# Storing the second one-hot of the PEER gate matrix token by token

## The chip, the cores and the metric

The kernel runs on one core of one Trainium2 chip. The metric is the device time of one execution in microseconds (us), from the chip's own clock. The engines are named as the profile names them: PE is TensorE's matrix multiply, PEld its loading of the stationary operand, DVE is VectorE, ACT is ScalarE, POOL is GpSimd, and SP is the engine that here only issues DMAs.

## The reference, cut to what matters

A decoder trunk of two layers (one recurrent, one with latent attention) runs over 512 tokens of width 1024. Each layer ends in a PEER block: every token picks 16 of 16384 tiny experts in each of 8 heads, and the result is a gated sum over the picked experts.

```python
def peer(h, w_q, sub_keys, u_tab, v_tab):
    q = (h @ w_q).reshape(B, S, PEER_HEADS, 2, PEER_HALF)
    s = jnp.einsum('bshpd,hpnd->bshpn', q, sub_keys)
    v1, i1 = lax.top_k(s[..., 0, :], 16); v2, i2 = lax.top_k(s[..., 1, :], 16)
    cand = v1[..., :, None] + v2[..., None, :]       # 16 x 16 per head
    cv, ci = lax.top_k(cand, 16)                      # of the 256
    idx = e1 * 128 + e2;  g = softmax(cv)             # e1, e2: the two key numbers
    act = gelu(h . u_tab[idx])
    return sum(g * act * v_tab[idx])
```

## The kernel before

The kernel does not gather rows for the first 384 tokens. It treats the block as two dense products over all 16384 experts (128 tiles of 128 experts), and multiplies the activations by a **gate matrix** that holds g where a token picked an expert and zero elsewhere. The last 128 tokens are done with gathered rows, in the background. Operands in fp32 are split in a high and a low part, and each product is three matmuls (lines 181, 182 and 183 of the helper `mm3`), so that most of the PE work is on these three lines.

A PEER block has these stages, once in each layer:

1. Queries, key scores and top-k (`pq`, `sc`, lines 914 to 942).
2. **The gate stage** (lines 945 to 978). The key numbers e1 and e2 of each block of 128 tokens are decoded (`decode`, lines 763 to 808, tiles `oh`, `ib`, `e`), transposed so that tokens lie along the free dimension (`gate_prep`, tiles `et`, `gp`), and then `gate_group` is called 24 times, once for 16 tokens each.
3. The V stage (lines 1029 to 1053): for each of 128 expert tiles the activations are weighted and multiplied by a tile of the value table into six accumulators (`acc`), while gathers for the last 128 tokens go on.

For one token the gate matrix over 128 x 128 key pairs is the product of two one-hot matrices over the 128 picks: rows of picks against key number e2 (**o2**, the stationary operand) and rows of picks against key number e1, times g (**pr**, the moving operand, in two fp16 parts). `gate_group` works on 16 tokens as two halves of eight (HT = 8). For each half VectorE makes

- `o1` (line 840): is key number equal to e1, for 128 keys and 8 tokens, 1024 fp16 elements in each partition;
- `pr[1]` (line 841): o1 times the low part of g, on VectorE in the first half and on GpSimd in the second;
- `o2` (line 842): is key number equal to e2;
- `pr[0]` (line 843): o1 times the high part of g.

The profile strips buffer numbers, so both one-hots are named `o` there and the line tells them apart. All four tiles have the shape [128, 2, 128, 4]: two groups, then keys, then four tokens **interleaved** as the innermost dimension. The instruction therefore reads the e2 of four neighbouring tokens as neighbouring elements, and compares them with a table `iota_e` in which each key number stands four times. TensorE then runs 16 matmuls for the half (line 848), each of 128 x 128 x 128 in fp16, and both of its operands step by four elements (8 bytes) from column to column. ScalarE copies each bank of four tokens to `stg` (line 851), and `stg` goes out to a DRAM scratch (line 853) from which the V stage reads it back.

Between the groups the program issues `u_part` (lines 888 to 905): a tile of the first table is loaded, split on ScalarE (line 161, `whi`) and GpSimd (line 162, `wlo`), multiplied on TensorE in 24 matmuls of 384 columns, and passed through GELU. Each call of `gate_group` is followed by the decode steps of later blocks. The last three `u_part` of the stage are held until the last gate matmul (lines 974 and 975).

The order of the instructions on each engine is not the order of the code: a scheduler sets it ahead of time from its own estimate of what each instruction costs. `o2` and `pr` have two buffers each, so VectorE can be two halves ahead of TensorE.

Of the kernel before, what the change touches and what calls it, by code (L numbers as in the profile page):

```python
# [12 lines left out]
F16 = mybir.dt.float16  # L13
# [3 lines left out]
OP = mybir.AluOpType  # L17
# [4 lines left out]
P = 128  # L22
# [16 lines left out]
TG = 16  # L39
# [8 lines left out]
HT = 8  # L48
# [31 lines left out]
class Trunk:  # L80
# [24 lines left out]
    def setup(self):  # L105
        nc, c, io = self.nc, self.consts, self.io
        self.csil = c.tile([P, D], F32, name="csil")
        nc.scalar.dma_start(self.csil, bass.AP(tensor=io["c"].tensor, offset=io["c"].offset, ap=[[0, P], [1, D]]))
        nc.scalar.activation(self.csil, self.csil, AF.Silu)
        self.x = self.state.tile([P, KC, T], F32, name="x")  # L110
        for k in range(0, KC, 2):
            nc.sync.dma_start(self.x[:, k:k + 2, :], io["xT"][:, k:k + 2, :])
        self.vecs = c.tile([P, NV], F32, name="vecs")
        nc.scalar.dma_start(self.vecs, io["vecs"])
        self.cst = c.tile([P, 4], F32, name="cst")
        nc.scalar.dma_start(self.cst, io["cst"])
        ii = c.tile([P, P], I32, name="ii")
        nc.gpsimd.iota(ii, pattern=[[1, P]], base=0, channel_multiplier=-1)
        self.ident = c.tile([P, P], F32, name="ident")
        nc.vector.tensor_scalar(self.ident, ii, 0.0, None, op0=OP.is_equal)  # L120
        self.ones = c.tile([P, 1], F32, name="ones")
        nc.vector.memset(self.ones, 1.0)
        self.iota_e = c.tile([P, P, 4], F16, name="iota_e")
        nc.gpsimd.iota(self.iota_e, pattern=[[1, P], [0, 4]], base=0, channel_multiplier=0,
                       allow_small_or_imprecise_dtypes=True)
        self.iota_m = c.tile([P, TOPK, TOPK], BF, name="iota_m")
        nc.gpsimd.iota(self.iota_m, pattern=[[1, TOPK], [0, TOPK]], base=0, channel_multiplier=0,
                       allow_small_or_imprecise_dtypes=True)
        self.eps = c.tile([P, 1], F32, name="eps")
        nc.vector.memset(self.eps, EPS)  # L130
        self.tiny = c.tile([P, 1], F32, name="tiny")
        nc.vector.memset(self.tiny, 1e-30)
        self.mod = c.tile([P, 112], F32, name="mod")
        self.xscr = self.dram.tile([P, KC, T], F32, name="xscr")
        self.gscr = self.dram.tile([DEPTH, SPILL, P, ND], F32, name="gscr")
        self.rscr = self.dram.tile([P, T], F32, name="rscr")
        self.mscr = self.dram.tile([P, NB, T], BF, name="mscr")
        self.wscr = self.dram.tile([DEPTH, NSG, P, P * TG], F32, name="wscr")
# [686 lines left out]
    def gate_group(self, pool, l, b, sg, et, gp):  # L825
        nc = self.nc
        n4 = HT // 4
        shp = [P, n4, P, 4]
        io = self.iota_e.unsqueeze(1).to_broadcast(shp)
        stg = pool.tile([P, P, TG], F32, name="stg", bufs=2)  # L830
        for t0 in range(0, TG, HT):

            def toks(ap):
                o = sg * TG + t0
                return ap[:, o:o + HT].rearrange("p (a t) -> p a t", t=4).unsqueeze(2).to_broadcast(shp)

            o2 = pool.tile(shp, F16, name="o2", bufs=2)
            o1 = pool.tile(shp, F16, name="o1", bufs=2)
            pr = [pool.tile(shp, F16, name=f"pr{q}", bufs=2) for q in range(2)]
            nc.vector.tensor_tensor(o1, io, toks(et[:, 0, :]), op=OP.is_equal)  # L840
            (nc.gpsimd if t0 else nc.vector).tensor_tensor(pr[1], o1, toks(gp[:, 1, :]), op=OP.mult)  # L841
            nc.vector.tensor_tensor(o2, io, toks(et[:, 1, :]), op=OP.is_equal)  # L842
            nc.vector.tensor_tensor(pr[0], o1, toks(gp[:, 0, :]), op=OP.mult)  # L843
            for a in range(n4):
                wps = self.bank("wps")
                for t in range(4):
                    for q in range(2):
                        last = nc.tensor.matmul(wps[:, t * P:t * P + P], o2[:, a, :, t], pr[q][:, a, :, t],  # L848
                                         start=q == 0, stop=q == 1)
                c = t0 + 4 * a  # L850
                nc.scalar.activation(stg[:, :, c:c + 4].rearrange("p e t -> p t e"),
                                     wps.rearrange("p (t e) -> p t e", t=4), AF.Copy, scale=1.0 / GSCALE)
        nc.scalar.dma_start(self.wscr[l, b * (P // TG) + sg], stg.rearrange("p e t -> p (e t)"))
        return last.ins
# [370 lines left out]
```

## Time and profile before

| | |
|---|---|
| median of three runs | 3260.37 us (3260.09 to 3264.49) |
| span of the profiled execution, first to last instruction | 3255.7 us |
| instructions | 43571 |
| mean granted TensorE clock | 0.967 |
| gate stage, layer 0 | about 490 to 727 us |
| V stage, layer 0 | about 727 to 1620 us |
| gate stage, layer 1 | about 2126 to 2367 us |
| V stage, layer 1 | about 2367 to 3222 us |

The span leaves out what lies ahead of the first and behind the last instruction: the median of the runs is 4.7 us longer than the profiled execution's span, and the profile gives no other time for that execution. "Busy" in the profile is the time from an instruction's start to its end, which includes time in which an engine that has started an instruction is held up inside it. A row of a timeline gives start, duration, engine, line, operation, and the tiles written and read. A row of a view by stages gives the stretch, its length, the busy time and number of instructions of PE, PEld, DVE, ACT and POOL, the granted clock, the DMA share and GB/s.

### The profile page before, as it was taken

To read this page: it belongs to the slowest core of one execution; us is meant where nothing else is said; L and a number is where in the kernel's file an instruction comes from. 1 tells how busy PE (TensorE), PEld (TensorE's weight loads), DVE (VectorE), ACT (ScalarE), POOL (GpSimd) and SP (SyncE) were. 2 spreads that over 40 slices of the span, in tenths; PEclk is the share of its full clock that TensorE was granted. 3 is DMA by queue.
4 is the path that set the end of the run, shared out by engine and by line. 5 is a ranking of instruction groups with operands and counts; after the bars stand their busy time and mean duration, and the time that the engine had idled before them with its cause. 6 is when DMAs were issued, how large, how long until landed. Compare 5 with 4: busy or idle time off the path is not lost. (4 is left out here: it accounts for less than half of the span.)

```text
span 3255.7 us, 43571 instructions
## 1 busy us (share of the span) xinstructions
PE 3027.2 (93%) x15486; PEld 2673.7 (82%) x15486; DVE 2721.5 (84%) x4924; ACT 1401.5 (43%) x1986; POOL 1491.7 (46%) x995
## 2 busy tenths in 40 slices
PE   6778879999999999999988989988999999999998
PEld 4657778898799999999766768878888899999997
DVE  8999999987688888888768968999956888888877
ACT  4543236653333333333456652356543333333333
POOL 5554455651044444444346645656510444444442
PEclk9888989999999999999989999989999999999999
DMA  6443445569899999999512333345698999999994
GB/s 249 147 162 130 145 148 180 186 225 344 274 359 350 328 335 337 349 336 326 178 36 84 100 110 130 112 176 183 218 313 257 315 350 328 336 333 344 341 333 175
DMA packets 319771, 786.55 MB, mean 242 GB/s; under 512 B 30785, under 2 KB 153793, under 8 KB 313153
## 3 DMA queue, kind: packets, MB, share of 16 engines
q1 hardware_dynamic: 226960, 443.61, 40.8%
q0 software_dynamic: 73728, 268.47, 23.1%
q10 hardware_dynamic: 18864, 71.69, 5.6%
q8 instruction: 122, 2.00, 0.2%
q14 instruction: 97, 0.79, 0.1%
HBM read 713.68 MB, written 69.99 MB: 241 GB/s over the span
## 5 line engine op out<-in xcount | busy, mean ns | idle before, releaser
L181 PE MATMUL u<-hh,wlo 128*128 128x384 f32 x2048 | 699.6, 342 | 19.8 <-ACT gact L905 13.2
L183 PE MATMUL u<-hh,whi 128*128 128x384 f32 x2048 | 697.8, 341 | 0.0
L182 PE MATMUL u<-hl,whi 128*128 128x384 f32 x2048 | 696.1, 340 | 0.0
L1110 POOL DMA_INDIRECT grow<-in_u_dram,idx x256 | 334.0, 1305 | 662.4 <-DVE gdot L1114 483.2
L162 POOL TENSOR_TENSOR wlo<-raw,whi 128x1024 fp32r<-128x1024 f32 (+2 forms) x211 | 481.0, 2285 | 271.7 <-ACT whi L161 261.4
L182 PE MATMUL acc<-vl,ah 128*128 128x512 f32 x1536 | 600.6, 391 | 2.3 <-DVE vl L162 2.3
L183 PE MATMUL acc<-vh,ah 128*128 128x512 f32 x1536 | 600.8, 391 | 0.0
L181 PE MATMUL acc<-vh,al 128*128 128x512 f32 x1536 | 592.0, 389 | 2.7 <-DVE mod L151 1.0
L162 DVE TENSOR_TENSOR vl<-vraw,vh 128x1024 fp32r<-128x1024 f32 x256 | 313.6, 1225 | 243.1 <-ACT vh L161 231.0
L1110 POOL DMA_INDIRECT grow<-in_v_dram,idx x256 | 329.1, 1285 | 380.2 <-DVE gacc L1119 259.0
L181 PEld LDWEIGHTS u<-hh,wlo 128*128 128x128 f32 x2048 | 392.9, 192 | 27.8 <-issue 14.0
L161 ACT ACTIVATE whi<-raw 128x1024 fp32r<-128x1024 f32 (+2 forms) x376 | 362.8, 966 | 118.2 <-PE acc L183 66.0
L182 PEld LDWEIGHTS u<-hl,whi 128*128 128x128 f32 x2048 | 392.1, 191 | 6.2
L183 PEld LDWEIGHTS u<-hh,whi 128*128 128x128 f32 x2048 | 391.8, 191 | 0.1
L181 PEld LDWEIGHTS acc<-vh,al 128*128 128x128 f32 x1536 | 288.4, 188 | 61.0 <-ACT vh L161 1.4
L183 PEld LDWEIGHTS acc<-vh,ah 128*128 128x128 f32 x1536 | 288.3, 188 | 60.2
L182 PEld LDWEIGHTS acc<-vl,ah 128*128 128x128 f32 x1536 | 288.3, 188 | 60.0 <-DVE vl L162 3.0
L1114 DVE CUSTOM_DVE_ANT_0 grow<-grow,hn 128x1024 f32<-128x1024 f32 x256 | 307.9, 1221 | 27.2 <-DMA grow<-in_u_dram,idx 26.6
L1119 DVE SCALAR_TENSOR_TENSOR gacc<-grow,gdot,gacc 128x1024 f32<-128x1024 f32 x254 | 325.2, 1280 | 5.5 <-DMA grow<-in_v_dram,idx 4.6
L161 ACT ACTIVATE ah<-gact 128x384 fp32r<-128x384 f32 x240 | 126.2, 526 | 467.8 <-DVE gact L997 327.2
L905 ACT ACTIVATE gact<-u 128x384 f32<-128x384 f32 x176 | 86.5, 491 | 494.0 <-PE u L183 487.6
L161 ACT ACTIVATE vh<-vraw 128x1024 fp32r<-128x1024 f32 x256 | 268.5, 1051 | 42.0 <-DMA vraw<-in_v_dram 23.5
(357 smaller groups left out, 5089.7 us busy)
## 6 DMA issues: line engine op xcount, KB each, us to landing
raw<-in_uT_dram SPq DMA_DIRECT2D x256, 512.0 KB
vraw<-in_v_dram SPq DMA_DIRECT2D x256, 512.0 KB
ada_raw<-in_adaw_dram SPq DMA_DIRECT2D x112, 512.0 KB
wscr<-stg ACTq DMA_DIRECT2D x48, 1024.0 KB
wt<-wscr SPq DMA_DIRECT2D x32, 1536.0 KB
raw<-in_w_pq_dram SPq DMA_DIRECT2D x32, 512.0 KB
gscr<-gsp ACTq DMA_DIRECT2D x64, 192.0 KB
gact<-gscr SPq DMA_DIRECT2D x64, 192.0 KB
```

The costliest lines, as they stand in the source:

```text
L161: nc.scalar.activation(hi, src, AF.Copy)
L162: return (eng or nc.vector).tensor_tensor(lo, src, hi.bitcast(F32), op=OP.subtract)
L181: nc.tensor.matmul(out, al, bh, start=first, stop=False)
L182: nc.tensor.matmul(out, ah, bl, start=False, stop=False)
L183: return nc.tensor.matmul(out, ah, bh, start=False, stop=last)
L905: nc.scalar.activation(gact[t], out[:, :ND], AF.Gelu)
L1110: nc.gpsimd.indirect_dma_start(out=row, out_offset=None, in_=tabs[s], in_offset=bass.IndirectOffsetOnAxis(ap=idx[:, k:k + 1], axis=0))
L1114: nc.vector.tensor_tensor_reduce(row, row, hn, op0=OP.mult, op1=OP.add, scale=1.0, scalar=0.0, accum_out=col)
L1119: nc.vector.scalar_tensor_tensor(acc, row, col, acc, op0=OP.mult, op1=OP.add)
```

## The change

The second one-hot is stored token by token: [128, 8, 128], tokens outside and the 128 key numbers inside. Each matmul then reads its stationary operand with a step of one element. A new table `iota_c` of [128, 128] holds each key number once. The comparison reads that table again for each token, and reads the e2 of one token again for all 128 keys. `o1` and `pr` stay interleaved by four.

```diff
+        self.iota_c = c.tile([P, P], F16, name="iota_c")
+        nc.gpsimd.iota(self.iota_c, pattern=[[1, P]], base=0, channel_multiplier=0,
+                       allow_small_or_imprecise_dtypes=True)
...
-            o2 = pool.tile(shp, F16, name="o2", bufs=2)
+            rows = [P, HT, P]
+            o2 = pool.tile(rows, F16, name="o2", bufs=2)
...
-            nc.vector.tensor_tensor(o2, io, toks(et[:, 1, :]), op=OP.is_equal)
+            o = sg * TG + t0
+            nc.vector.tensor_tensor(o2, self.iota_c.unsqueeze(1).to_broadcast(rows),
+                                    et[:, 1, o:o + HT].unsqueeze(2).to_broadcast(rows), op=OP.is_equal)
...
-                        last = nc.tensor.matmul(wps[:, t * P:t * P + P], o2[:, a, :, t], pr[q][:, a, :, t],
+                        last = nc.tensor.matmul(wps[:, t * P:t * P + P], o2[:, 4 * a + t, :], pr[q][:, a, :, t],
                                           start=q == 0, stop=q == 1)
```

In the changed kernel the lines stand at other numbers: `o1` is line 844, `pr[1]` 845, `o2` 847, `pr[0]` 849, the matmul 854, and `wlo` 165.

## The prediction

> **What bounds the kernel now.** I read the view by stages first, over the stretches in which the changed lines run: the two gate stages, each cut where PE stops having idle time, and the second V stage behind them.
>
> ```profile
> 490.00:686.00 196.00, 176.94 (x1165) 170.18 (x1164) 188.64 (x230) 124.85 (x146) 116.25 (x51) 0.93 0.53 187
> 686.00:727.00 41.00, 40.83 (x281) 39.04 (x280) 34.76 (x28) 25.68 (x30) 23.88 (x10) 1.00 0.67 249
> 2126.00:2307.00 181.00, 158.04 (x1057) 151.16 (x1055) 174.40 (x210) 115.76 (x135) 110.33 (x45) 0.94 0.54 188
> 2307.00:2367.00 60.00, 59.64 (x403) 57.12 (x404) 46.28 (x47) 36.04 (x42) 37.29 (x17) 0.97 0.64 228
> 2367.00:3222.00 855.00, 855.00 (x4212) 764.03 (x4211) 672.47 (x854) 313.88 (x425) 321.17 (x253) 1.00 0.93 322
> ```
>
> In the first and third row PE (first busy column) leaves 19 and 23 us idle, and DVE (third) leaves only 7 us idle in each. In the second and fourth row it is the other way round: PE is full and DVE has 6 and 14 us free. In the last row PE is busy all the time, so a microsecond that the gate stage ends later is a microsecond later at the end. DMA is at 0.53 to 0.67 in the gate stages and bounds nothing there.
>
> The waits of layer 0's stage say whom PE waits for, and the chain that ended last, in order of time, says the same for layer 1 (start, length, engine and line):
>
> ```profile
> PEld L848 <- DVE o L842: 22.4, 13, 6.0
> PE wps L848 <- DVE o L842: 18.5, 11, 5.7
> ```
>
> ```profile
> 2294.32 0.61 DVE o L842
> 2294.93 0.60 DVE o L840
> ...
> 2306.70 0.61 DVE o L842
> 2307.36 2.06 PE wps L848 x16
> ```
>
> The gate matmuls wait for the very instruction that the change touches, and the chain runs along DVE until 2307 us and then along PE. The steps of 0.60 us are the pace of these DVE instructions when nothing holds them up.
>
> But DVE's busy time is not all work. The timeline shows what is in it:
>
> ```profile
> 2187.47 0.68 DVE L842 TENSOR_TENSOR o<-iota_e,et 128x1024 f16<-128x1024 f16 x1
> 2187.87 2.54 POOL L162 TENSOR_TENSOR wlo<-raw,whi 128x1024 fp32r<-128x1024 f32 x1 [2.67 <-ACT whi L161]
> 2188.07 2.89 DVE L840 TENSOR_TENSOR o<-iota_e,et 128x1024 f16<-128x1024 f16 x1
> 2191.10 2.21 POOL L841 TENSOR_TENSOR pr<-o,gp 128x1024 f16<-128x1024 f16 x1 [0.69 <-DVE o L840]
> 2191.48 2.38 DVE L841 TENSOR_TENSOR pr<-o,gp 128x1024 f16<-128x1024 f16 x1
> ```
>
> The DVE instruction at 2188.07 takes 2.89 us where its twin took 0.68: the POOL instruction ends at 2190.41, and DVE ends 0.55 us after it. The same again at 2191.48. So in this stage **DVE and POOL take turns**, one instruction at a time. The shortest of each form show their work without the turn-taking (duration as min/median/max in ns):
>
> ```profile
> L842 DVE TENSOR_TENSOR o<-iota_e,et x96: 677/680/2876, 490.9 to 2358.1; 128x1024 f16<-128x1024 f16 x96
> L841 POOL TENSOR_TENSOR pr<-o,gp x48: 1889/2212/6026, 496.9 to 2357.6; 128x1024 f16<-128x1024 f16 x48
> L162 POOL TENSOR_TENSOR wlo<-raw,whi x28: 2385/2685/6450, 492.8 to 721.3; 128x1024 fp32r<-128x1024 f32 x28
> ```
>
> I add up layer 1's stage by turns. DVE makes 168 one-hots and products (48 + 48 + 48 + 24) at 0.60 = 101 us. POOL makes 24 products at 1.89 = 45 us and some 29 splits at 2.39 = 69 us. The decode's `oh` instructions, about 2.1 us for each of 10 steps by the same pace (an estimate), are 21 us. The sum is 236 us of the 241 between 2126 and 2367. So the stage is filled by these two engines' turns, and the PE-full tails are about full of turns too.
>
> **The change part by part.**
>
> *o2 on DVE, 96 instructions.* The amount of data stays, 1024 fp16 elements. What changes is that one operand now repeats a single element 128 times, and no row of the trace has that on DVE. It is bounded by 0.68 us (the pace is kept) and by the nearest form of as many elements without pairs, a split in fp32:
>
> ```profile
> L162 DVE TENSOR_TENSOR vl<-vraw,vh x256: 1217/1226/1289, 728.9 to 3220.9; 128x1024 fp32r<-128x1024 f32 x128
> L162 DVE TENSOR_TENSOR vl<-v,vh x8: 654/680/692, 1662.6 to 1817.8; 128x512 fp32r<-128x512 f32 x8
> L162 DVE TENSOR_TENSOR yl<-tanh,yh x4: 679/1222/2865, 165.7 to 230.5; 128x512 fp32r<-128x512 f32 x4
> ```
>
> 512 elements of four bytes take 0.680 us, exactly as long as 1024 of two bytes. So DVE moves one 4-byte word per step, and two fp16 neighbours ride in one word. A repeated element has no neighbour to ride with, so I take the unpaired price, 1.226 us: **+0.546 us each**. The third row excludes that the slow form escapes the turns: its 512 fp32 elements take up to 2.87 us. [...]
>
> *Where the 96 lie.* The view by stages for line 842 alone counts them:
>
> ```profile
> 490.00:686.00 196.00, 36.04 (x40) 0.93 0.53 187
> 686.00:727.00 41.00, 7.14 (x8) 1.00 0.67 249
> 2126.00:2307.00 181.00, 28.43 (x36) 0.94 0.54 188
> 2307.00:2367.00 60.00, 16.98 (x13) 0.97 0.64 228
> ```
>
> 76 lie where DVE and POOL alone set the pace: 76 x 0.546 = **+41.5 us**. The other 20 lie in the tails: at most 20 x 0.546 = 10.9 us more, at least nothing if they all fit into the 20 us that DVE has free there. In the compiled order of the changed program PE's `u` matmuls come earlier (29 to 32 between two groups where there were 25 to 28), and the last three to four groups of each layer have none between them. PE then no longer fills the tails, and the turns set the pace to the end. I take 7.5 of the 10.9 us, since some gaps there can be filled.
>
> *The matmuls, 1536 of them.* Their number, columns and moving operand stay. The weight load is a possible gain:
>
> ```profile
> L848 PEld LDWEIGHTS <-o x1536: 112/117/146, 497.4 to 2365.3; 128*128 128x128 f16 x192
> 2234.48 3.96 PE wps L848 x32
> ```
>
> 32 matmuls take 3.96 us with their drain, so about 118 ns from one to the next, as long as one load. The moving operand still steps by 8 bytes, and either may set that pace. The ends are no gain at all and half a load, 59 ns; a loss I exclude, since the same columns are read from neighbouring addresses. The upper end is 1536 x 59 = 91 us of PE time, but in the early stretches PE waits for o2 anyway and only waits longer, and in the tails it is no longer the bound. I count **0**, covered by the turns of DVE and POOL; if that cover were gone (the pairing kept), the 355 gate matmuls of the tails (147 + 208) could give at most 355 x 59 = 21 us. [...]
>
> *The rest.* The iota costs less than its larger sister's 1.20 us (row below), at 1 us into the span, behind the first loads: nothing. `toks` loses one use, at no cost at run time. On SP two `u` loads move ahead of the first read-back of `wscr`, with DMA half free. Behind the slower o2 on DVE wait `pr[0]`, the next o1 and the decode, and POOL's `wlo` and `pr[1]` wait for their turn; that is the cost already counted.
>
> ```profile
> L124 POOL IOTA iota_e<- x1: 1197/1197/1197, 1.0 to 1.0; 128x512 f16 x1
> ```
>
> *Sum.* 41.5 + 7.5 = **+49 us**: the profiled span would go from 3255.7 to 3304.7, and with the 4.7 us by which the median stands above the span, the predicted time is 3260.4 + 49 = **3309 us**.
>
> **The rivals.**
>
> *A. Part of the turns is slack.* If POOL's records are longer than what they really hold (its spans are rough), DVE can slip into the difference. For it: 5 us of layer 1's stage are not in my sum. Against it: DVE ends 0.55 us after POOL each time. With half the price hidden, 96 x 0.546 / 2 = +26: 3286 us.
>
> *B. The pairing is kept*, because the repeated operand costs nothing. Then the edit does not do to DVE what I say, and PE waits as before: 3260 us. For it: no row of the trace has the case.
>
> *C. Faster.* The pairing is kept, and the load halves. Early stretches stay as they are, and the full-PE tails shrink. It decides only if o2 stays under about 0.68 us plus DVE's free 20 us over 20 instructions in the tails. The price is at most -21 us, and about half of that, since DVE then catches up as the bound: 3250 us. Against it: two things must both go well.
>
> *D. The clock falls as well.* With no `u` work between the last groups PE is sparse, and its clock may drop just as the 72 held `u` matmuls of a layer begin. The trace has such a drop:
>
> ```profile
> 527.73 0.52 PE L181 MATMUL u<-hh,wlo 128*128 128x384 f32 x1
> 528.05 0.52 PE L182 MATMUL u<-hl,whi 128*128 128x384 f32 x1
> ...
> 549.02 0.33 PE L183 MATMUL u<-hh,whi 128*128 128x384 f32 x1
> 549.19 0.34 PE L181 MATMUL u<-hh,wlo 128*128 128x384 f32 x1
> ```
>
> 0.32 us from one to the next against 0.17: 72 x 0.15 = 11 us for each layer, if it lasts for all of them, so 3309 + 22 = 3331 us.
>
> **How the numbers follow.** Forecast (turns, full price, 3301 to 3319) 0.75; A 0.10; B 0.05; C 0.03; D 0.07. The likeliest is 3309. Without B, C, the upper half of D and the outer parts of the forecast and A, some 2 in 10 are left out: the range is 3286 to 3326. It holds both ends of the unknown tail cost (3302 and 3313). About 0.2%, 6.5 us, is what a measurement of this kernel can tell from no change: faster 0.03 (C), same 0.05 (B), slower 0.92.
>
> **What would show it.** Line 847 should have a median near 1.22 us and line 844 still 0.68. Both gate stages should be longer, by 21 to 26 us each, and nothing else. DVE should be on the chain to the end of the stage, and PE's waits for o2 should grow. If line 847 stays at 0.68 us, the price was wrong (B or C). If it is 1.22 us but the stages grow by less than 15 us each, the turns had slack (A). If the `u` matmuls behind the last gate matmul take 0.32 us from one to the next, it is D. If the gate matmuls come at less than 118 ns, the load did set their pace, and the question is whether any of it reached the end.

## The result, and the profile after

The change made the kernel slower: 3313.45 us (median of 4 runs, 3312.96 to 3316.28) against 3260.23 us for the kernel before (4 runs, 3259.43 to 3264.49). The ratio is 1.0162, 95% interval 1.0148 to 1.0176, a loss of 53 us. The profiled span is 3312.1 us where it was 3255.7, which is 56 us more. The execution profiled here took 3313.88 us, 1.8 us more than its span, and so did the later runs of the kernel before (3261.48 for a span of 3259.7). So the 4.7 us between span and median ahead of the change are for the most part a profiled execution that was some 3 us quicker than the median; a difference from that span is too large by as much.

First the view by stages of the kernel after: both gate stages, the last 41 and 60 us of each (as long as the tails that the prediction cut off), and the second V stage. Columns as before: length, then PE, PEld, DVE, ACT and POOL.

```profile
493.00:752.00 259.00, 215.62 (x1412) 205.16 (x1410) 247.50 (x260) 149.74 (x174) 156.90 (x60) 0.86 0.51 181
711.00:752.00 41.00, 28.62 (x215) 26.46 (x213) 39.30 (x39) 22.36 (x25) 22.18 (x10) 0.73 0.56 205
2156.00:2421.00 265.00, 224.07 (x1454) 213.17 (x1453) 240.26 (x257) 152.13 (x177) 173.64 (x62) 0.87 0.52 182
2361.00:2421.00 60.00, 46.83 (x321) 43.95 (x319) 54.01 (x49) 31.57 (x36) 38.85 (x16) 0.82 0.60 210
2434.00:3291.00 857.00, 857.00 (x4209) 763.61 (x4208) 671.91 (x852) 312.21 (x423) 318.54 (x252) 1.00 0.92 317
```

From the first `o` to the last gate matmul, layer 0's stage took 232.6 us before (490.3 to 722.9) and takes 258.5 after (493.4 to 751.8, from rounded ends); layer 1's took 239.8 (2125.6 to 2365.4) and takes 264.6 (2156.2 to 2420.8). That is +25.9 and +24.8, together **+50.7 us**. The V stage of layer 1, from its first `acc` matmul to its last, took 856.9 us before and 857.0 after. So the loss lies in the two stages that use the edited instruction. A few microseconds more stand ahead of layer 0's gate stage, which began 3.1 us later. No edited instruction but the iota lies there, a run without the iota began 2.4 us later too (the first experiment, 492.7), and the four runs of the kernel before spread over 5 us.

PE filled the tails before. Now it is busy for only 28.6 of 41 and 46.8 of 60 us there, and DVE is the fuller engine.

The view of the tile `o` gives the price (min/median/max in ns):

```profile
L854 PEld LDWEIGHTS <-o x1536: 95/116/148, 499.0 to 2420.7; 128*128 128x128 f16 x192
L844 DVE TENSOR_TENSOR o<-iota_e,et x96: 674/678/2891, 493.4 to 2414.9; 128x1024 f16<-128x1024 f16 x96
L847 DVE TENSOR_TENSOR o<-iota_c,et x96: 1207/1211/3439, 494.0 to 2415.5; 128x1024 f16<-128x1024 f16 x96
```

o1 (line 844) is as it was; o2 (line 847) has a median of 1.211 us, **0.533 us more** than o1. 96 x 0.533 = 51.2 us, which is the growth of the two stages within half a microsecond. The timeline of DVE and POOL shows the new form in the turns:

```profile
2395.67 2.69 POOL L165 TENSOR_TENSOR wlo<-raw,whi 128x1024 fp32r<-128x1024 f32 x1 [1.32 <-ACT whi L164]
2396.04 3.41 DVE L847 TENSOR_TENSOR o<-iota_c,et 128x1024 f16<-128x1024 f16 x1
2398.33 2.87 POOL L845 TENSOR_TENSOR pr<-o,gp 128x1024 f16<-128x1024 f16 x1
2399.37 2.38 DVE L844 TENSOR_TENSOR o<-iota_e,et 128x1024 f16<-128x1024 f16 x1
2402.27 1.21 DVE L847 TENSOR_TENSOR o<-iota_c,et 128x1024 f16<-128x1024 f16 x1
```

The first o2 starts 0.37 us after POOL, lasts 3.41 us and ends 1.09 us after POOL's end at 2398.36. The second, with POOL done, lasts 1.21 us. POOL's product, started at 2398.33, ends at 2401.20, 2.87 us later where its shortest took 1.89: this time POOL was held by DVE.

The waits of layer 0's gate stage stand against 22.4 and 18.5 us in the kernel before:

```profile
PEld L854 <- DVE o L847: 30.7, 18, 5.5
...
PE wps L854 <- DVE o L847: 25.4, 16, 5.1
```

One sign that the prediction named cannot be read. The chain of the kernel after goes back only to 2419.01 us, just ahead of the last 16 gate matmuls, so it does not say whether VectorE was on it before. These matmuls themselves waited 2.02 us for VectorE (`pr`, line 849; the row stands in the part on the rivals).

### The profile page after: what moved, and what is told of

Same layout as the page of the kernel before. It is cut to its first block, busy times and chain, and to the rows that moved or that the text cites. A ratio compares the mean times of both kernels' runs of the same rounds, so it can differ in the third digit from the quotient of the medians.

```text
span 3312.1 us, 43563 instructions
## 1 busy us (share of the span) xinstructions
PE 3038.8 (92%) x15486; PEld 2684.6 (81%) x15486; DVE 2766.5 (84%) x4924; ACT 1401.3 (42%) x1986; POOL 1527.0 (46%) x996
## 3 DMA queue, kind: packets, MB, share of 16 engines
q0 software_dynamic: 73728, 268.47, 22.8%
## 5 line engine op out<-in xcount | busy, mean ns | idle before, releaser
L165 POOL TENSOR_TENSOR wlo<-raw,whi 128x1024 fp32r<-128x1024 f32 (+2 forms) x211 | 493.1, 2343 | 241.1 <-ACT whi L164 232.8
```

Of the source, the lines that this page charges most:

```text
L165: return (eng or nc.vector).tensor_tensor(lo, src, hi.bitcast(F32), op=OP.subtract)
```

## The experiments

The theory (1): the repeated operand nearly doubles o2's time on VectorE, and since VectorE and GpSimd take turns, the 96 extra half microseconds reach the end. Rivals: (2) the new layout, or the new order of instructions, costs the time; (3) VectorE alone is the bound, and GpSimd has no part in it; (4) the stationary operand's step sets TensorE's pace in the gate matmuls; (5) that pace decides the time of the whole stage. "Stage" below is the stretch from the first `o` to the last gate matmul, layer 0 / layer 1. Ratios are against runs of the kernel before that were taken beside each experiment (medians 3261 to 3264 us), with their 95% intervals.

### The price without the layout

```diff
 # kernel before; o2 stays interleaved
-            nc.vector.tensor_tensor(o2, io, toks(et[:, 1, :]), op=OP.is_equal)
+            o = sg * TG + t0
+            nc.vector.tensor_tensor(o2, io, et[:, 1, o:o + n4].unsqueeze(2).unsqueeze(3).to_broadcast(shp), op=OP.is_equal)
```

> The kernel before with its interleaved o2 and strided matmuls, but the comparison reads one token's e2 512 times in a row in place of four tokens' in turn (o2 then holds the wrong tokens). Only the repeated operand of the change is in it. Theory 1: o2 at about 1.21 us, time 3308 to 3318 us, as the whole change. Rival 2 (layout, unit step or order carry part of it): clearly less than 3300 us.

Measured: 3314.59 us, ratio 1.0156 (1.0141 to 1.0170), stages 259.8 / 263.2 us. The tile view of this run, where line 843 is o2:

```profile
L843 DVE TENSOR_TENSOR o<-iota_e,et x96: 1210/1215/3425, 493.3 to 2415.5; 128x1024 f16<-128x1024 f16 x96
```

The whole loss is there, with the old layout, the old table and the old step of the stationary operand. The repeated element alone makes it.

### The layout without the price

```diff
 # changed kernel; the comparison no longer reads e2
             nc.vector.tensor_tensor(o2, self.iota_c.unsqueeze(1).to_broadcast(rows),
-                                    et[:, 1, o:o + HT].unsqueeze(2).to_broadcast(rows), op=OP.is_equal)
+                                    self.iota_c.unsqueeze(1).to_broadcast(rows), op=OP.is_equal)
```

> The changed kernel, but o2 is compared with a constant table instead of e2 (its values are then wrong): the token-by-token layout and the unit step of the stationary operand stay, no operand repeats an element, and ScalarE has nothing to do with it. Theory 1 (the lost pairing is the whole loss): o2 at 0.68 us, 3255 to 3268 us, and what the expansion on ScalarE kept of the loss was its own cost. Rival 2 (layout or order): 3278 to 3290 us, as with the expansion on ScalarE.

Measured: 3262.49 us, ratio 0.9997 (0.9987 to 1.0008). Line 847 of this run:

```profile
L847 DVE TENSOR_TENSOR o<-iota_c x96: 676/680/2854, 462.9 to 2363.2; 128x1024 f16<-128x1024 f16 x96
```

With a unit step on both operands o2 takes 0.680 us again, and with it the loss is gone, in the new layout. The layout as a cause falls (rival 2). One reservation: o2 no longer waits for `et` here, so the order is not quite that of the changed kernel.

### The turns: GpSimd's products moved to VectorE

The 48 `pr[1]` that run on GpSimd (shortest 1.89 us) go to VectorE, where they take 0.60 in the turns; once in the changed kernel and once in the kernel before.

```diff
-            (nc.gpsimd if t0 else nc.vector).tensor_tensor(pr[1], o1, toks(gp[:, 1, :]), op=OP.mult)
+            nc.vector.tensor_tensor(pr[1], o1, toks(gp[:, 1, :]), op=OP.mult)
```

> The changed kernel with pr[1] of the second half on VectorE too, not on GpSimd: 24 instructions of each layer move from 1.89 us on GpSimd to 0.60 us on VectorE. Theory 1 (VectorE and GpSimd take turns, and their sum is the stage): each stage shrinks by 24 x 1.29 = 31 us, time about 3251 us (3245 to 3262). Rival 3 (VectorE alone is the bound, and GpSimd works beside it): each stage grows by 24 x 0.60 = 14 us, time about 3342 us.

Measured for the changed kernel: 3262.39 us, ratio 1.0000 (0.9990 to 1.0010), stages 235.7 / 231.0 us. The view by stages:

```profile
493.00:729.00 236.00, 207.90 (x1411) 198.92 (x1409) 212.09 (x284) 150.32 (x174) 124.83 (x35) 0.90 0.55 194
2130.00:2362.00 232.00, 214.13 (x1452) 205.31 (x1451) 209.84 (x281) 152.27 (x179) 128.54 (x35) 0.94 0.56 197
```

VectorE has 24 instructions more in each layer, and the kernel is 51 us faster than the changed one. If VectorE alone were the bound, it would have become slower, by 48 x 0.60 = 29 us; that rival (3) falls. The gain is below the 48 x (1.89 - 0.60) = 62 us of the turns, and the time 11 us above the 3251 that theory 1 named: layer 1's stage gained 33.6 us where 31 were due, and layer 0's 22.8. Why layer 0 gave less was not tried. Some 6 us of the stages' gain were lost behind them in layer 1: from the last gate matmul to the first `acc` matmul it is 17.2 us where the changed kernel has 13.5, and the V stage is 2 us longer.

> The kernel before with pr[1] of the second half on VectorE too. Theory 1: each stage could shrink by 31 us, but TensorE has only 19 and 23 us of idle time in them, so that it becomes the bound: 3215 to 3232 us. Rival 3: about 3260 + 2 x 14 = 3289 us, or less where VectorE has idle time, but not below 3255 us.

Measured for the kernel before: 3214.53 us, ratio 0.9848 (0.9834 to 0.9863), stages 212.2 / 217.6 us: 48 us faster, just below the range that theory 1 named.

```profile
494.00:707.00 213.00, 208.06 (x1421) 201.06 (x1420) 196.65 (x281) 149.92 (x175) 119.87 (x36) 0.98 0.61 217
2104.00:2322.00 218.00, 214.57 (x1454) 208.29 (x1453) 194.07 (x281) 150.75 (x177) 110.50 (x38) 0.97 0.61 219
```

The group of gate matmuls (busy us, mean ns, then idle us before them), first in the kernel before, then in this run:

```profile
L848 PE MATMUL wps<-pr,o 128*128 128x128 f16 x1536 | 194.1, 297 | 42.6 <-DVE o L842 38.6 <-DVE pr L841 2.8 <-POOL pr L841 1.0
```

```profile
L848 PE MATMUL wps<-pr,o 128*128 128x128 f16 x1536 | 191.9, 297 | 6.8 <-DVE o L842 4.0 <-DVE pr L841 2.7
```

Its idle time falls from 42.6 to 6.8 us. PE is busy for 208 of 213 and 214.6 of 218 us; it is the bound now, which is why the gain stops at 48 of 62 us.

```diff
 # the same, and the split of the low part in the gate stage also on VectorE
-                        u_part(nc.gpsimd)
+                        u_part(nc.vector)
```

> The kernel before with pr[1] and, for the u tiles issued between the gate groups, also the split wlo on VectorE: in each layer 24 products go from 1.89 to 0.60 us and about 26 splits from 2.39 to 1.15 us. Theory 1: the turns of a stage sum to about 240 - 31 - 32 = 177 us, so TensorE is the bound with its 214 to 218 us of busy time less what a steadier clock gives back: 3205 to 3228 us, not slower than the version with pr[1] alone moved. Rival 3: VectorE's work grows by 14 + 30 us for each layer and it alone is the bound: slower than 3260 us.

Measured: 3216.97 us, ratio 0.9862 (0.9847 to 0.9877), stages 218.1 / 213.4 us.

```profile
487.00:706.00 219.00, 202.97 (x1402) 194.22 (x1401) 181.27 (x309) 150.96 (x174) 14.39 (x12) 0.93 0.59 208
2108.00:2323.00 215.00, 206.16 (x1419) 196.88 (x1418) 178.51 (x306) 151.93 (x175) 41.47 (x9) 0.94 0.60 211
```

GpSimd's busy time falls from 120 to 14 us in layer 0, and nothing is gained over the run before: its turns were no longer the bound. PE leaves 16 and 9 us idle here, and VectorE more. In layer 0 PE's weight loads waited 15.2 us for `pr` (line 843), and the `pr` instructions 16.0 us for gate matmuls; what would shorten the stage further was not tried.

The same run shows the turns most directly:

```profile
L842 DVE TENSOR_TENSOR o<-iota_e,et x96: 675/686/890, 487.6 to 2319.6; 128x1024 f16<-128x1024 f16 x96
```

The longest o2 takes 0.89 us here, where the kernel before has up to 2.876 with the same instruction. Of VectorE's one-hots and products in the gate stages, 64 of 336 took over 1.5 us in the kernel before, 33 of 384 with the products taken off GpSimd, and 3 of 384 here. The long VectorE instructions go when GpSimd's work goes.

### What the step costs TensorE

Three edits of the kernel before replace the step of 8 bytes by a unit step, without any change on VectorE. A matmul then reads 128 neighbouring elements, that is, parts of several tokens' one-hots; the number and size of the matmuls stay.

```diff
+            fl = lambda x, j: x.rearrange("p a e t -> p (a e t)")[:, j * P:j * P + P]
 # stationary only:  matmul(..., fl(o2, 4 * a + t), pr[q][:, a, :, t], ...)
 # moving only:      matmul(..., o2[:, a, :, t], fl(pr[q], 4 * a + t), ...)
 # both:             matmul(..., fl(o2, 4 * a + t), fl(pr[q], 4 * a + t), ...)
```

> The kernel before, whose matmuls read the stationary operand as 128 neighbouring elements of the interleaved o2 (so of mixed tokens); nothing changes on VectorE. It is the TensorE half of the change alone. Theory 1: gate matmuls still come about 116 to 118 ns apart, since the moving operand sets the pace, and the time is 3255 to 3263 us. Rival 4 (the stationary operand's step sets the pace): 60 to 90 ns apart, and up to 21 us faster through the tails: 3239 to 3255 us.

Measured: 3260.12 us, ratio 0.9991 (0.9981 to 1.0001), stages 232.0 / 239.2 us.

```profile
L849 PEld LDWEIGHTS <-o x1536: 95/115/146, 497.1 to 2364.3; 128*128 128x128 f16 x192
```

The shortest load falls from 112 to 95 ns, its median only from 117 to 115, and the matmuls still come 115 to 116 ns apart. The load follows the matmuls; it does not set their pace, so rival 4 falls.

> The kernel before, whose matmuls read the moving operand as 128 neighbouring elements (mixed tokens), the stationary one still at a step of four. Theory 1 (the moving operand's step of 8 bytes sets the pace): 55 to 90 ns apart. Rival 4: still 117 ns. The time changes little either way, at most 21 us less, because VectorE and GpSimd set the pace of the early stretches: 3239 to 3262 us.

Measured: 3264.57 us, ratio 1.0006 (0.9997 to 1.0016), stages 233.3 / 240.7 us. Tile view, and the group of the gate matmuls:

```profile
L849 PEld LDWEIGHTS <-o x1536: 110/114/152, 499.4 to 2374.6; 128*128 128x128 f16 x192
L849 PE MATMUL wps<-pr,o x1536: 216/219/330, 499.4 to 2374.6; 128*128 128x128 f16 x192
```

```profile
L849 PE MATMUL wps<-pr,o 128*128 128x128 f16 x1536 | 126.1, 248 | 103.3 <-DVE o L842 95.3 <-POOL pr L841 4.8 <-DVE pr L841 2.8
```

Now the pace changes. Where the granted clock is full, it is 55 to 56 ns (median) from one matmul to the next instead of 117. TensorE's busy time for them falls from 194.1 us (kernel before) to 126.1, by 68 us. The idle time before them grows from 42.6 to 103.3 us, by 61, and nearly all of it ends with o2. TensorE only waits longer: the time is that of the kernel before (and 2.6 us above the range expected).

> The kernel before, with both matmul operands read as 128 neighbouring elements (mixed tokens). If each operand alone can hold the pace at 117 ns, only this one is faster: 55 to 85 ns apart. Theory 1 on the time: still 3239 to 3262 us, since some 20 us in the tails are all that TensorE can give. Rival 5 (TensorE's pace counts in the whole stage): 1536 x 50 ns = 77 us less, 3183 us.

Measured: 3261.35 us, ratio 0.9998 (0.9989 to 1.0007), stages 232.9 / 237.1 us.

```profile
L849 PEld LDWEIGHTS <-o x1536: 95/98/152, 497.8 to 2366.4; 128*128 128x128 f16 x192
```

The load's median now falls to 98 ns, and the pace is that of the run before (32 matmuls in 1.96 us, 1.98 there). So the step of the moving operand sets the pace, and no gain on TensorE reaches the end while the turns are the bound.

### Repetition moved to ScalarE

ScalarE writes e2 out 128 times, and VectorE compares two operands with unit step.

```diff
 # changed kernel
-            nc.vector.tensor_tensor(o2, self.iota_c.unsqueeze(1).to_broadcast(rows),
-                                    et[:, 1, o:o + HT].unsqueeze(2).to_broadcast(rows), op=OP.is_equal)
+            nc.scalar.activation(o2, et[:, 1, o:o + HT].unsqueeze(2).to_broadcast(rows), AF.Copy)
+            nc.vector.tensor_tensor(o2, self.iota_c.unsqueeze(1).to_broadcast(rows), o2, op=OP.is_equal)
```

> The changed kernel, but ScalarE first writes each token's e2 128 times into o2 and VectorE compares in place, so that no operand of VectorE repeats an element; the token-by-token layout and the unit step of the stationary operand stay. Theory 1 (the whole loss is the lost pairing on VectorE, taken in turns with GpSimd): o2 falls back to a median of about 0.68 us, both gate stages to about 233 and 240 us, the time to 3255 to 3268 us; ScalarE's 48 x 1.06 = 51 us more for each layer fit beside its 150 of 259 us. Rival 2 (the layout or the new order of the instructions costs part of it): the time stays above 3285 us though o2 is back at 0.68 us.

Measured: 3284.57 us, ratio 1.0069 (1.0055 to 1.0083), stages 247.4 / 249.9 us.

```profile
L848 ACT ACTIVATE o<-et x96: 1039/1070/1137, 488.6 to 2387.4; 128x1024 f16<-128x1024 f16 x96
...
L849 DVE TENSOR_TENSOR o<-iota_c,o x96: 676/680/7517, 491.7 to 2388.5; 128x1024 f16<-128x1024 f16 x96
```

The pairing is back (0.680 us), but by the ratio some 22 us of the loss stay, so this missed the time that the pairing alone gives, and just missed the rival's. ScalarE writes into o2, which TensorE must first have released: a suspect. In the next kernel the copy has a tile of its own.

```diff
+            eb = pool.tile(rows, F16, name="eb", bufs=1)
-            nc.scalar.activation(o2, et[:, 1, o:o + HT].unsqueeze(2).to_broadcast(rows), AF.Copy)
-            nc.vector.tensor_tensor(o2, self.iota_c.unsqueeze(1).to_broadcast(rows), o2, op=OP.is_equal)
+            nc.scalar.activation(eb, et[:, 1, o:o + HT].unsqueeze(2).to_broadcast(rows), AF.Copy)
+            nc.vector.tensor_tensor(o2, self.iota_c.unsqueeze(1).to_broadcast(rows), eb, op=OP.is_equal)
```

> The expansion of e2 on ScalarE again, but into a tile of its own with one buffer, where the first version wrote it into o2 and so had to wait for TensorE to release o2. If that wait was what the first version lost: 3258 to 3272 us. If ScalarE's place in its queue, behind the copies of the gate banks, was: 3278 us or more.

Measured: 3271.48 us, ratio 1.0026 (1.0017 to 1.0036), stages 238.9 / 246.0 us. So some 13 of the 22 us go with the copy's own tile. That it was the wait for o2's release is likely and not shown: the views of waits book ScalarE's waits for PE to its copies of the gate banks (`stg`, 49.5 us over both stages in the first version and 2.2 here), none to its write into o2. PE's waits for o2 fall from 65.5 to 41.7 us. The rest, some 9 us over the run without the price, is not settled; VectorE's o2 waits 7.8 us for the copies `eb` here, and ScalarE has 48 of them, of 1.06 us, more in its queue in each layer, but whether that costs the time was not tried.

### The roles exchanged

The unit step shortens the matmuls on the moving side. So o2 and pr exchange places: the one-hot of e1, stored token by token, is the moving operand, and the weighted, interleaved one-hot of e2 the stationary one. `pr[1]` is on VectorE, as in the turns experiments.

```diff
 # changed kernel
-            nc.vector.tensor_tensor(o1, io, toks(et[:, 0, :]), op=OP.is_equal)
-            (nc.gpsimd if t0 else nc.vector).tensor_tensor(pr[1], o1, toks(gp[:, 1, :]), op=OP.mult)
+            nc.vector.tensor_tensor(o1, io, toks(et[:, 1, :]), op=OP.is_equal)
+            nc.vector.tensor_tensor(pr[1], o1, toks(gp[:, 1, :]), op=OP.mult)
...
-                                    et[:, 1, o:o + HT].unsqueeze(2).to_broadcast(rows), op=OP.is_equal)
+                                    et[:, 0, o:o + HT].unsqueeze(2).to_broadcast(rows), op=OP.is_equal)
...
-                        last = nc.tensor.matmul(wps[:, t * P:t * P + P], o2[:, 4 * a + t, :], pr[q][:, a, :, t],
+                        last = nc.tensor.matmul(wps[:, t * P:t * P + P], pr[q][:, a, :, t], o2[:, 4 * a + t, :],
```

> The same product with the roles exchanged: the one-hot of e2 is interleaved, weighted with g and stationary, the one-hot of e1 is stored token by token and is the moving operand; pr[1] all on VectorE. It pays the price of the change once, and the gate matmuls should come 55 to 107 ns apart as in the run with a unit step of the moving operand alone. Theory 1 (turns of VectorE and GpSimd): as the changed kernel with pr[1] on VectorE, 3255 to 3268 us. Rival 5 (TensorE's pace counts): clearly faster, 3225 us or less.

Measured: 3273.64 us, ratio 1.0030 (1.0016 to 1.0044), stages 243.2 / 236.2 us.

```profile
L847 DVE TENSOR_TENSOR o<-iota_c,et x96: 1174/1216/3433, 491.5 to 2368.1; 128x1024 f16<-128x1024 f16 x96
L854 PE MATMUL wps<-o,pr x1536: 216/219/330, 498.0 to 2372.2; 128*128 128x128 f16 x192
```

The matmuls run at the short pace (56 ns), and the time is not below that of the changed kernel with `pr[1]` on VectorE (3262.39), which has the same work on VectorE and GpSimd. A pace of TensorE that decides (rival 5) falls again. It is 11 us above that run and 6 above the range of theory 1 (its six runs lie between 3264 and 3276); this was not explained.

```diff
 # the same, and
-                        u_part(nc.gpsimd)
+                        u_part(nc.vector)
```

> The exchanged roles, with pr[1] and the splits wlo between the gate groups on VectorE. Theory 1: the turns of a stage sum to about 177 + 26 = 203 us, TensorE's work to about 214 - 768 x 0.045 = 180 us, so a stage takes 203 to 210 us where the version without the exchange took 218 and 213: 3195 to 3212 us, the fastest of all. If handing over between the two engines bounds it and not either's work: 3213 us or more.

Measured: 3207.94 us, ratio 0.9830 (0.9814 to 0.9847), stages 212.8 / 206.6 us.

```profile
487.00:701.00 214.00, 173.68 (x1394) 164.76 (x1393) 200.41 (x305) 146.14 (x170) 24.00 (x11) 0.82 0.60 214
2099.00:2312.00 213.00, 179.55 (x1438) 170.44 (x1437) 204.55 (x308) 151.55 (x178) 20.74 (x11) 0.86 0.62 220
```

Here GpSimd has almost nothing left, VectorE is the bound with 200 of 214 us, and PE has 40 and 33 us to spare. It has the lowest time of all, 53 us below the kernel before. Its interval overlaps that of the kernel before with `pr[1]` on VectorE alone (0.9834 to 0.9863), so the simple edit, one line, may be nearly as good.

## Why the prediction was right

The forecast was 3309 us; 3313.45 were measured, and the mechanism held. That the growth came so close is in part luck: the price was 1.2 us too large over 96 instructions, the tails were counted 3.4 us too low, and the two errors have opposite signs.

**What bounds the kernel: right.** The gate stages' growth went through the V stage to the end unchanged, since that stage took 857 us either way. That VectorE and GpSimd take turns was read from the trace alone in the prediction; the runs that took 48 products off GpSimd show it, at -51 and -48 us, and the long VectorE instructions disappear with GpSimd's work (64, 33 and 3 of them).

**The price of o2: right in kind, 2% too large in size.** It was to go from 0.680 to 1.226 us (+0.546), and the run has 1.211 against 0.678 (+0.533). The nearest row, a split in fp32, was a fair price. With the old layout and an operand that repeats one element, o2 took 1.215 us (the price alone); with the new layout and no repeated operand it took 0.680 (the paired constant). That two fp16 elements ride in one 4-byte word is the author's reading of such times: the runs show the times alone.

**Where the 96 lie: the mis-sized term.** The 76 in the early stretches were to cost 41.5 us, and the 20 in the tails 7.5 of at most 10.9, since some gaps there could be filled. The tails hid nothing: the stages grew by 50.7 us and 96 x 0.533 is 51.2. Of the prediction's own reasons the one that counted is that PE would no longer fill the tails; the two tail rows of the kernel after show it idle for 12 and 13 us. So the full price was due on all 96, and 49 us became 51. The last 2 us up to the 53 of the medians are not explained; the medians of the kernel before themselves lie between 3260 and 3264 us.

**The matmuls: counted at nothing, rightly; its bound for the tails was wrong.** The prediction left open which operand sets the pace of 118 ns. It is the moving one, which this change doesn't touch. If the pairing had been kept, it allowed up to 21 us of gain in the tails. The runs with a paired o2 and unit steps gained none: 0.9998 (0.9989 to 1.0007) with both operands. "PE is full" in a tail did not mean that PE had all of it to give. In the kernel before the last o2 starts only 4.2 us ahead of the last gate matmul in layer 0 (718.7 and 722.9) and 7.3 in layer 1 (2358.1 and 2365.4), and only this much is PE's while VectorE keeps its pace. With both unit steps VectorE kept it: the last o2 starts 228.9 and 232.3 us behind the first one-hot, where it was 228.4 and 232.5. Layer 1's stage became 2.7 us shorter and layer 0's did not.

The moving operand in fp16 ran at 117 ns from one matmul to the next at a step of 8 bytes and, at the full clock, at 55 to 56 at unit step. For the stationary operand the load's median went from 114 to 98 ns in the runs with a unit-step moving operand.

**The rivals.** A, half the price hidden in slack (3286), falls: nothing was hidden. B, the pairing kept (3260), and C, faster (3250), fall with the row of line 847; the run with the paired constant shows that B would have given its time, and the run with the unit-step stationary operand that C would not have come even so. D, the clock that falls at the held `u` matmuls (3331), came true in its cause and failed in its size. PE was busy for 4.4 of the 9.4 us from 2410.0 to 2419.4, at a granted clock of 0.50. The timeline of PE in the kernel after, at the end of layer 1's gate stage:

```profile
2419.06 2.02 PE L854 MATMUL wps<-pr,o 128*128 128x128 f16 x16 [2.02 <-DVE pr L849]
2420.83 0.67 PE L184 MATMUL u<-hh,wlo 128*128 128x384 f32 x1
...
2422.57 0.42 PE L186 MATMUL u<-hh,whi 128*128 128x384 f32 x1
2422.83 0.34 PE L184 MATMUL u<-hh,wlo 128*128 128x384 f32 x1
2423.01 0.34 PE L185 MATMUL u<-hl,whi 128*128 128x384 f32 x1
```

The first six `u` matmuls (five in layer 0) come 0.32 us apart and the others at 0.17 to 0.18: 6 x 0.15, about 1 us in each layer, not 72 x 0.15 = 11. The granted clock is 0.50 from 2419.4 to 2422.7 us and 1.00 from 2422.8 on.

## What to carry to other kernels

An operand that repeats one 2-byte element along the innermost dimension made a VectorE comparison 1.8 times as long (0.678 to 1.211 us); ahead of such a change of layout, see which engine bounds the stage that has to make the operand. Add up VectorE's and GpSimd's elementwise work as one sum, for in these stages they ran one at a time (64 of 336 VectorE instructions took over 1.5 us beside GpSimd's work, 3 of 384 with most of it moved away): a product took 1.89 us on GpSimd and 0.60 on VectorE, and each of the 48 that moved saved about 1 us of the kernel's time (51 and 48 us), until TensorE became the bound. On TensorE look at the step of the moving operand before that of the stationary one (117 to 56 ns from one matmul to the next at the full clock, against 118 to 116), and only where TensorE's work reaches the end.

## What the runs showed of the hardware that was not expected

- The step of the moving operand, 8 bytes against 2, halved the pace of these matmuls with 128 columns in fp16 at the full clock: 117 ns against 55 to 56. The step of the stationary one hardly touched it (118 against 116 ns, medians, before and after the change).
- At the 8-byte step, a lower clock did not show in the gate matmuls; at the unit step it did. Sorted by the granted clock, the kernel before has a median of 118 ns from one to the next at 1.0 and at 0.5, the run with the unit-step moving operand 56 ns at 1.0 and 107 at 0.5. So at the lower clock the unit step gained little. The timeline of that run has 16 of them in 1.08 us (clock 1.00), and the next 16 in 1.64 us, in which the clock falls (0.50 from 579.3 to 582.6 us), and the `u` matmuls behind them are long too:

```profile
577.05 1.08 PE L849 MATMUL wps<-pr,o 128*128 128x128 f16 x16 [1.24 <-DVE o L842]
578.87 1.64 PE L849 MATMUL wps<-pr,o 128*128 128x128 f16 x16 [0.73 <-DVE o L842]
580.27 0.67 PE L182 MATMUL u<-hl,whi 128*128 128x384 f32 x1
580.74 0.52 PE L183 MATMUL u<-hh,whi 128*128 128x384 f32 x1
```

  In the changed kernel, with the 8-byte step, 16 took 2.02 us just ahead of the `u` matmuls at 0.32 us (the fence above), about the pace that the kernel before had at full clock (32 in 3.96).
- A dropped clock was back after 3.5 to 3.7 us of matmuls without a gap: in the kernel after PE had no idle time from 750.11 us on, and the `u` matmuls came at the full pace from 753.6; in layer 1 from 2419.06 on, and from 2422.8.
